# Softmax minus one-hot on one core: whole stores in two transfers, and the load behind them held until the first has landed

## The chip, the cores and the metric

The kernel runs on one core of a Trainium2 chip. The metric is the device time of one execution in microseconds (us). A difference between kernels is measured by running both on the same chip.

## The reference

The input is a batch of logits, 8 x 1024 rows of 8192 float32 values, and one label for each row. For each row the softmax is computed and 1 is subtracted at the label (the gradient of the cross entropy):

```python
def reference(logits, labels):                      # (8, 1024, 8192) f32, (8, 1024) i32
    logits_max = np.max(logits, axis=-1, keepdims=True)
    exp_logits = np.exp(logits - logits_max)
    softmax = exp_logits / np.sum(exp_logits, axis=-1, keepdims=True)
    ...
    one_hot[batch_idx, seq_idx, labels] = 1.0
    return (softmax - one_hot).astype(np.float32)
```

268 MB are read and 268 MB are written.

## The kernel before

The 8192 rows are cut into `B` = 32 batches of 256 rows. A batch has two rows in each of the 128 partitions (`G` = 2), and these two rows follow one another in memory, so that each partition's share of a batch is one run of 64 KB. The buffer `X` has three slots (`SLOTS`) of one batch each. A batch is computed in its slot and stored from it.

For each row t of 64 (`T`, two per batch), VectorE takes the negated maximum (`row_max`), ScalarE the exponentials in place with their sum (`exponentials`), VectorE the reciprocal and, in one instruction, the product less the one-hot row (`finish`). The one-hot row stands as bytes in the PSUM tile `hot`, which ScalarE writes with two instructions per row (`mark`), the first of them through the tile `away`. TensorE only transposes the labels at the start.

Semaphores and their waits are written by hand. The helper `run` (its instructions carry line 77) puts every wait but the last on the engine ahead of the instruction, and the last on the instruction itself. All loads and stores are issued by SyncE, in the order of the program, and go into one queue: `load(b)` waits until the store of batch b - 3, which used the same slot, has landed; `store(b)` waits until the batch's rows are finished.

The strings `LOADS` and `STORES` say for each batch whether it moves row by row ("r", two transfers of 4 MB) or whole ("w", one transfer of 8 MB). The loads of batches 6 to 30 and the stores of batches 3 to 27 are whole. The last batch is stored in four transfers of 2 MB.

The main loop computes batch b, issues its store, and then issues the next load. After batch 3 (`EARLY`) it issues none, so that from then on the load behind store b is that of batch b + 2; its slot was that of batch b - 1. After batch 27 (`LATE`) it issues two.

```python
        for b in range(B):
            work(b)
            store(b)
            if b == EARLY:
                continue
            for _ in range(2 if b == LATE else 1):
                if nxt < B:
                    load(nxt)
                    nxt += 1
```

A transfer over 128 partitions is spread over 16 DMA engines, and its semaphore has its full count when all 16 have landed their share.

Of the kernel before, what the change touches and what calls it, by code (L numbers as in the profile page):

```python
# [8 lines left out]
G = 2  # L9
SLOTS = 3  # L10
EARLY = 3
LATE = 27

LOADS = "rrrrrrwwwwwwwwwwwwwwwwwwwwwwwwwr"
STORES = "rrrwwwwwwwwwwwwwwwwwwwwwwwwwrrrr"
# [3 lines left out]
def kernel(  # L19
# [6 lines left out]
    nc = tc.nc  # L26
# [10 lines left out]
    N, V = x_nv.shape  # L37
# [5 lines left out]
    o_b = o_nv.rearrange("(b p j) v -> b p j v", p=P, j=G)  # L43
# [4 lines left out]
    X = const.tile([P, SLOTS, G, V], fp32)  # L48
# [16 lines left out]
    with tc.tile_critical():  # L65
        sem = tc.alloc_semaphore
        got = [[sem(f"got{i}{q}") for q in range(4)] for i in range(SLOTS)]
        put = [[sem(f"put{i}{q}") for q in range(4)] for i in range(SLOTS)]
# [3 lines left out]
        def run(engine, waits, counter, method, **operands):  # L72

            waits = list(dict.fromkeys(waits))
            for w in waits[:-1]:
                engine.wait_ge(*w)
            instruction = getattr(engine, method)(**operands)  # L77
            for w in waits[-1:]:
                instruction._wait_ge(*w)
            step = 16 if method == "dma_start" else 1  # L80
            instruction.then_inc(counter, step)
            count[counter.name] = count.get(counter.name, 0) + step
            return counter, count[counter.name]

        every, rows = slice(0, P), slice(0, G)
# [7 lines left out]
        def meets(a, b):  # L93
            sets = [[set(range(*d.indices(n))) for d, n in zip(p, (P, G))] for p in (a, b)]
            return all(x & y for x, y in zip(*sets))

        loaded, stored, sides_done = {}, {}, {}
        maxed, summed, marked, finished, freed = {}, {}, {}, {}, {}

        def load(b):  # L100
            loaded[b] = []
            before = stored.get(b - SLOTS, [])
            for q, piece in enumerate(PIECES[LOADS[b]]):
                ps, js = piece
                free = [w for other, w in before if meets(piece, other)]
                w = run(
                    nc.sync, free, got[b % SLOTS][q], "dma_start",
                    out=X[ps, b % SLOTS, js, :], in_=x_b[b, ps, js, :],
                )
                loaded[b].append((piece, w))  # L110

        def store(b):
            stored[b] = []
            if b == B - 1:
                for t in (T - G, T - 1):
                    j = t % G
                    for i, cs in enumerate(sides):
                        w = run(
                            nc.sync, [sides_done[t][i]], put[b % SLOTS][G * j + i],
                            "dma_start", out=o_b[b, every, one[j], cs], in_=X[every, b % SLOTS, one[j], cs],  # L120
                        )
                        stored[b].append(((every, one[j]), w))
                return
            for q, piece in enumerate(PIECES[STORES[b]]):
                ps, js = piece
                w = run(
                    nc.sync, [finished[b * G + js.stop - 1]], put[b % SLOTS][q], "dma_start",
                    out=o_b[b, ps, js, :], in_=X[ps, b % SLOTS, js, :],
                )
                stored[b].append((piece, w))  # L130
# [47 lines left out]

        w_raw = run(nc.scalar, [], lab_got, "dma_start", out=lab_raw[:], in_=lab_bp)
        for b in range(SLOTS):  # L180
            load(b)
        w = run(nc.gpsimd, [], pool, "memset", ap=ident[:], constant=0.0)
        w_ident = run(
            nc.gpsimd, [w], pool, "affine_select",
            out=ident[:], in_=ident[:], compare_op=Alu.not_equal, fill=1.0,
# [8 lines left out]
        for j in range(G):  # L194
            w = run(
                nc.tensor, [w_ident, w_lab], pe, "transpose",
                out=lab_ps[:, j, :], in_=lab_f[:, j, :], identity=ident[:],
            )
        w = run(nc.vector, [w], dve, "tensor_copy", out=lab[:], in_=lab_ps)
        w = run(  # L200
            nc.vector, [w], dve, "tensor_scalar",
            out=part[:], in0=lab[:], scalar1=2, scalar2=None, op0=Alu.arith_shift_right,
        )
        w_word = run(
            nc.vector, [w], dve, "tensor_scalar",
            out=word[:], in0=part[:], scalar1=-1.0, scalar2=None, op0=Alu.mult,
        )
        w = run(
            nc.vector, [w_word], dve, "tensor_scalar",
            out=lab[:], in0=lab[:], scalar1=3, scalar2=None, op0=Alu.bitwise_and,  # L210
        )
        w = run(
            nc.vector, [w], dve, "tensor_copy", out=minus[:], in_=lab[:]
        )
        powers = [256.0**k for k in range(4)]
        w = run(
            nc.vector, [w], dve, "tensor_scalar",
            out=unit[:], in0=minus[:], scalar1=0.0, scalar2=powers[0], op0=Alu.is_equal, op1=Alu.mult,
        )
        for k in (1, 2, 3):  # L220
            w = run(
                nc.vector, [w], dve, "tensor_scalar",
                out=part[:].bitcast(fp32), in0=minus[:], scalar1=float(k),
                scalar2=powers[k], op0=Alu.is_equal, op1=Alu.mult,
            )
            w = run(
                nc.vector, [w], dve, "tensor_tensor",
                out=unit[:], in0=unit[:], in1=part[:].bitcast(fp32), op=Alu.add,
            )
        made_dve = run(  # L230
            nc.vector, [w], dve, "tensor_scalar",
            out=minus[:], in0=unit[:], scalar1=-1.0, scalar2=None, op0=Alu.mult,
# [4 lines left out]
        def work(b):  # L237
            t0, t1 = b * G, b * G + 1
            row_max(t0)
            exponentials(t0)  # L240
            if b == 0:
                mark(0)
                mark(1)
            row_max(t1)
            exponentials(t1)
            finish(t0)
            mark(t0 + G)
            finish(t1)
            mark(t1 + G)

        nxt = SLOTS
# [4 lines that stand above are left out]
                continue  # L256
            for _ in range(2 if b == LATE else 1):
                if nxt < B:
                    load(nxt)
                    nxt += 1  # L260
        for b in range(B - SLOTS, B):
            for _, w in stored[b]:
# [31 lines left out]
```

## Time and profile before

| | |
|---|---|
| median of 3 runs | 1264.38 us (1263.45 to 1265.66) |
| profiled execution | 1262.39 us, its span 1260.6 us |
| VectorE busy | 1120.2 us (89%) |
| ScalarE busy | 722.7 us (57%) |
| DMA queue of loads and stores | 99.5% of 16 engines' span |
| data moved | 426 GB/s over the span |

Busy time is what an engine's instructions took; waits are not in it. The DMA share is the time that the queue's packets took, as a share of the span of all 16 engines. In rows of stretches of time, the columns are the stretch and its width in us, the busy us and instructions of TensorE, its weight load, VectorE, ScalarE and GpSimd, the granted TensorE clock, the DMA engines' share and GB/s. Bytes and the time of a packet are counted in the stretch in which it starts, so that in stretches narrower than a packet the share can be over 1. In rows of instructions in order of time, the columns are start, duration, engine, line and instruction, with the idle time before it and what ended that in brackets. "SPq" is SyncE's queue of DMA issues.

### The profile page before, as it was taken

The numbers are of one execution on the slowest core, as the hardware profiler recorded it, in microseconds if no ns is written. First come the engines' busy times: TensorE is split into PE (matmuls) and PEld (weight loads), VectorE is DVE, ScalarE is ACT, GpSimd is POOL, SyncE is SP. The second block draws the span as 40 slices with busy tenths as digits, with TensorE's granted clock in tenths as the row PEclk, the third lists the DMA queues.
The fourth block names the chain that finished last, engine by engine and source line by source line (L and its number), as shares of the span: only waits on it lengthen the run. The fifth ranks groups of instructions, "written<-read, shape, count | busy, mean of one in ns | idle before, by whom it ended". The sixth has DMA issues, their size and how long they took to land.

```text
span 1260.6 us, 747 instructions
## 1 busy us (share of the span) xinstructions
PE 0.4 (0%) x2; PEld 0.3 (0%) x2; DVE 1120.2 (89%) x208; ACT 722.7 (57%) x257; POOL 2.3 (0%) x7
## 2 busy tenths in 40 slices
PE   0000000000000000000000000000000000000000
PEld 0000000000000000000000000000000000000000
DVE  6899999688988889888898888988889888898995
ACT  3666676356655575545755547555475554755662
POOL 0000000000000000000000000000000000000000
DMA  9999999999999999999999999999999999999998
GB/s 401 416 433 433 434 448 433 430 433 430 433 430 433 433 420 416 430 433 433 416 443 406 433 433 433 412 420 433 433 433 401 430 433 433 433 433 400 435 432 368
DMA packets 11574, 536.99 MB, mean 426 GB/s; under 512 B 1296, under 2 KB 1296, under 8 KB 1328
## 3 DMA queue, kind: packets, MB, share of 16 engines
q1 hardware_dynamic: 11520, 536.88, 99.5%
q10 hardware_dynamic: 48, 0.07, 0.0%
q14 instruction: 6, 0.05, 0.0%
HBM read 268.50 MB, written 268.44 MB: 426 GB/s over the span
## 4 chain that ended last, share of the span: by engine, by line
DVE 50%; DMA 43%; issue 4%; ACT 2%; SPq 0%
DMA X<-in_logits_dram 43%; DVE X L77 25%; DVE m L77 25%; ACT X L77 1%; DVE r L77 1%; ACT hot L77 0%; SPq L77 0%; ACT away L77 0%; SPq L289 0%; SPq L65 0%
## 5 line engine op out<-in xcount | busy, mean ns | idle before, releaser
L77 DVE TENSOR_REDUCE m<-X 128x1 f32<-128x8192 f32 x64 | 553.0, 8680 | 114.3 <-DMA X<-in_logits_dram 114.3
L77 ACT ACTIVATE X<-X,m 128x8192 f32<-128x8192 f32 x64 | 455.8, 7122 | 308.6 <-DVE m L77 308.6
L77 DVE SCALAR_TENSOR_TENSOR X<-X,r,hot 128x8192 f32<-128x8192 f32 (+1 forms) x66 | 560.1, 8489 | 3.8 <-ACT hot L77 1.6
L77 ACT ACTIVATE away<-count,word 128x2048 bf16<-128x2048 int16 x64 | 128.1, 2001 | 199.1 <-DVE X L77 148.1
L77 ACT ACTIVATE hot<-away,unit,minus 128x2048 int32<-128x2048 bf16 x64 | 131.9, 2061 | 2.1
L77 DVE RECIPROCAL r<-s 128x1 f32<-128x1 f32 x64 | 9.9, 155 | 2.4 <-ACT X L77 2.4
L77 ACT ACTIVATION_READ_ACCUMULATOR X<-X,m 128x1 f32 x64 | 11.9, 186 | 0.0
L77 DVE CAST lab_f<-lab_raw 32x256 f32<-32x256 int32 x1 | 0.4, 372 | 4.9 <-DMA lab_raw<-in_labels_dram 4.9
L77 ACT ACT_TABLE_LOAD x1 | 1.3, 1283 | 3.2 <-POOL count L77 3.2
L77 POOL IOTA count<- 128x2048 int16 x1 | 1.8, 1823 | 0.0
L77 DVE TENSOR_TENSOR unit<-unit,part 128x64 f32<-128x64 f32 x3 | 0.7, 224 | 0.1
L77 DVE CAST lab<-hot 128x64 int32<-128x64 f32 x1 | 0.2, 225 | 0.5 <-PE hot L77 0.5
L77 DVE TENSOR_SCALAR part<-minus 128x64 f32<-128x64 f32 x3 | 0.6, 195 | 0.1
L77 PE MATMUL hot<-ident,lab_f 32*128 32x32 f32 x2 | 0.4, 302 | 5.3 <-DVE lab_f L77 5.3
L77 PEld LDWEIGHTS hot<-ident,lab_f 32*128 32x128 f32 x2 | 0.3, 196 | 5.3 <-DVE lab_f L77 5.3
L77 DVE TENSOR_SCALAR part<-lab 128x64 int32<-128x64 int32 x1 | 0.2, 196 | 0.0
L77 DVE TENSOR_SCALAR word<-part 128x64 f32<-128x64 int32 x1 | 0.2, 195 | 0.0
L77 DVE TENSOR_SCALAR lab<-lab 128x64 int32<-128x64 int32 x1 | 0.2, 195 | 0.0
L77 DVE CAST minus<-lab 128x64 f32<-128x64 int32 x1 | 0.2, 195 | 0.0
L77 DVE TENSOR_SCALAR unit<-minus 128x64 f32<-128x64 f32 x1 | 0.2, 195 | 0.0
L77 DVE TENSOR_SCALAR minus<-unit 128x64 f32<-128x64 f32 x1 | 0.2, 195 | 0.0
L77 POOL TENSOR_SCALAR_AFFINE_SELECT ident<-ident 32x32 f32<-32x32 f32 x1 | 0.2, 203 | 0.1
(5 smaller groups left out, 0.5 us busy)
## 6 DMA issues: line engine op xcount, KB each, us to landing
X<-in_logits_dram SPq DMA_DIRECT2D x14, 4096.0 KB, 19.4
out_dram<-X SPq DMA_DIRECT2D x12, 4096.0 KB, 29.5
out_dram<-X SPq DMA_DIRECT2D x4, 2048.0 KB, 12.2
out_dram<-X SPq DMA_DIRECT2D x25, 23.7
X<-in_logits_dram SPq DMA_DIRECT2D x25, 43.1
lab_raw<-in_labels_dram ACTq DMA_DIRECT2D x1, 64.0 KB, 4.0
```

The source lines that it names most:

```text
L77: instruction = getattr(engine, method)(**operands)
```

## The change

Each whole store goes as two transfers over all partitions: the first takes a partition's 16,384 values but the last 2,048, the second takes those. The load that is issued behind a whole store waits, besides what it waited for, until the first of these two transfers has landed on all engines. Loads behind stores by rows wait for nothing more than before.

```diff
+LAST = 2048
...
-        def load(b):
+        def load(b, behind):
             loaded[b] = []
             before = stored.get(b - SLOTS, [])
+            gate = [stored[behind][0][1]] if stored and STORES[behind] == "w" else []
             for q, piece in enumerate(PIECES[LOADS[b]]):
                 ps, js = piece
                 free = [w for other, w in before if meets(piece, other)]
                 w = run(
-                    nc.sync, free, got[b % SLOTS][q], "dma_start",
+                    nc.sync, free + gate, got[b % SLOTS][q], "dma_start",
                     out=X[ps, b % SLOTS, js, :], in_=x_b[b, ps, js, :],
                 )
...
+            if STORES[b] == "w":
+                src = X[:, b % SLOTS].rearrange("p j v -> p (j v)")
+                dst = o_b[b].rearrange("p j v -> p (j v)")
+                cut = G * V - LAST
+                for q, cs in enumerate([slice(0, cut), slice(cut, G * V)]):
+                    w = run(
+                        nc.sync, [finished[b * G + G - 1]], put[b % SLOTS][q], "dma_start",
+                        out=dst[:, cs], in_=src[:, cs],
+                    )
+                    stored[b].append(((every, rows), w))
+                return
...
         for b in range(SLOTS):
-            load(b)
+            load(b, 0)
...
                 if nxt < B:
-                    load(nxt)
+                    load(nxt, b)
```

## The prediction

> **What bounds the kernel now.** I began with the page: its first line, the busy line, the DMA queue, the chain that ended last, and the issues.
>
> ```profile
> span 1260.6 us, 747 instructions
> PE 0.4 (0%) x2; PEld 0.3 (0%) x2; DVE 1120.2 (89%) x208; ACT 722.7 (57%) x257; POOL 2.3 (0%) x7
> q1 hardware_dynamic: 11520, 536.88, 99.5%
> DVE 50%; DMA 43%; issue 4%; ACT 2%; SPq 0%
> out_dram<-X SPq DMA_DIRECT2D x25, 23.7
> X<-in_logits_dram SPq DMA_DIRECT2D x25, 43.1
> ```
>
> The chain names DVE first, but the queue that carries all loads and stores is occupied for 99.5% of the span, and DVE has 11% left. A load lands 43.1 us after its issue and a store 23.7 us: the load stands behind the store in the same queue and two transfers pass before it lands. So the 25 stores and 25 loads of 8 MB (the rows without a size; 128 partitions x 64 KB) are the stage to read. Next I listed VectorE's groups in the stretch of whole transfers, then SyncE's and VectorE's instructions in order of time.
>
> ```profile
> L77 DVE TENSOR_REDUCE m<-X 128x1 f32<-128x8192 f32 x42 | 362.9, 8681 | 90.5 <-DMA X<-in_logits_dram 90.5
> ...
> 238.16 17.28 DVE L77 TENSOR_REDUCE m<-X 128x1 f32<-128x8192 f32 x2 [10.11 <-DMA X<-in_logits_dram]
> 276.78 17.28 DVE L77 TENSOR_REDUCE m<-X 128x1 f32<-128x8192 f32 x2 [3.64 <-DMA X<-in_logits_dram]
> ...
> 512.13 17.28 DVE L77 TENSOR_REDUCE m<-X 128x1 f32<-128x8192 f32 x2 [3.73 <-DMA X<-in_logits_dram]
> 552.27 17.28 DVE L77 TENSOR_REDUCE m<-X 128x1 f32<-128x8192 f32 x2 [5.15 <-DMA X<-in_logits_dram]
> 591.00 17.28 DVE L77 TENSOR_REDUCE m<-X 128x1 f32<-128x8192 f32 x2 [3.74 <-DMA X<-in_logits_dram]
> ...
> 1102.44 8.69 DVE L77 TENSOR_REDUCE m<-X 128x1 f32<-128x8192 f32 x1 [4.07 <-DMA X<-in_logits_dram]
> ```
>
> The first row counts 42 maxima from 276 to 1102 us, so 21 batches of two rows. Each batch starts when its load lands: (1102.44 - 276.78) / 21 = 39.32 us per batch, of which VectorE waits 90.5 / 21 = 4.3. The batch from 238.16 to 276.78 took only 38.62; others took 40.14 (512.13 to 552.27). As 128 partitions go to 16 DMA engines, each engine moves 8 pieces of 64 KB per transfer, 16 per batch: 38.62 / 16 = 2.41 us a piece. That is the unstalled rate, and the kernel loses 0.70 us per batch against it.
>
> To see where, I asked for narrow stretches of time. There GB/s times width, over 65,536 B, counts the pieces that start.
>
> ```profile
> 548.78:549.15 0.37, 0.00 (x0) 0.00 (x0) 0.00 (x0) 0.37 (x1) 0.00 (x0) 1.00 5.74 2480
> 549.15:551.15 2.00, 0.00 (x0) 0.00 (x0) 0.00 (x0) 1.97 (x2) 0.00 (x0) 1.00 0.00 0
> 551.15:551.60 0.45, 0.00 (x0) 0.00 (x0) 0.00 (x0) 0.16 (x1) 0.00 (x0) 1.00 4.70 2039
> 551.60:551.85 0.25, 0.00 (x0) 0.00 (x0) 0.00 (x0) 0.00 (x0) 0.00 (x0) 1.00 0.00 0
> 551.85:551.95 0.10, 0.00 (x0) 0.00 (x0) 0.00 (x0) 0.00 (x0) 0.00 (x0) 1.00 3.03 1311
> ...
> 587.90:588.10 0.20, 0.00 (x0) 0.00 (x0) 0.00 (x0) 0.20 (x1) 0.00 (x0) 1.00 0.00 0
> 588.10:588.30 0.20, 0.00 (x0) 0.00 (x0) 0.00 (x0) 0.20 (x1) 0.00 (x0) 1.00 12.36 5243
> ```
>
> 2480 x 0.37 is 14 pieces; 1311 x 0.10 is 2. Fourteen engines pass from the load to the store at about 549.0; two follow at 551.9, some 2.9 us later, and the load counts as landed only then (VectorE starts at 552.27). The other 2.9 us are worthless to the kernel: fourteen engines run ahead, and pay it back waiting, as at 587.90, where nothing starts until the store issued at 587.29 brings sixteen pieces at once.
>
> **The split.** 25 stores become a transfer of 14,336 columns and one of 2,048, a share of 1/8: per engine 8 pieces of 56 KB, then 8 of 8 KB. No row shows 8 KB pieces. The nearest are the last stores of the kernel, in pieces of 16 KB, against pieces of 32 KB just before:
>
> ```profile
> 1193.00:1207.50 14.50, 0.00 (x0) 0.00 (x0) 14.43 (x5) 11.28 (x4) 0.00 (x0) 1.00 1.01 434
> 1241.08:1255.64 14.56, 0.00 (x0) 0.00 (x0) 5.43 (x2) 0.00 (x0) 0.00 (x0) 1.00 1.00 430
> ```
>
> 434 to 430 is 1%, some 6 ns on a 605 ns piece. Eight more pieces per engine cost 0.05 us a store, 25 x 0.05 = 1.2 us. Bounds: nothing (the difference is partly the edges of the stretches), or four times as much. I take 0.05, the row's own. By the Trainium skill, "DMA: Bandwidth & Descriptors", section "Bandwidth", a 1 MB transfer takes 6.15 us and 16 MB run at 425 GB/s; by that table the tail of 1 MB would cost about 3.7 us more per store, 92 us in all, as an estimate. The trace speaks against it for a queue that is already running: stores of 2 MB pass back to back at 430. The second store instruction on SyncE adds a third of a microsecond there, while the queue still holds work.
>
> **The wait.** Load b+2 was issued right behind store b. Now SyncE holds it until the first part has landed on all sixteen engines. Behind the waiting load on SyncE stands only store b+1, due a batch (39 us) after store b; the wait ends some 21 us after it, so no store is late. The later double issue, after batch 27, already waits for a whole store. ACT and VectorE issue nothing behind it.
>
> The price is a hole in the queue if the way from "first part written" to "load's first piece" is longer than the tail, 19.3 / 8 = 2.4 us. The early stretch, where transfers go by single rows (32 KB pieces), shows this way:
>
> ```profile
> 82.50 0.34 SPq L77 DMA_DIRECT2D X<-in_logits_dram  x1
> 111.19 0.34 SPq L77 DMA_DIRECT2D X<-in_logits_dram  x1
> 150.29 10.24 SPq L77 DMA_DIRECT2D X<-in_logits_dram  x2
> ...
> 80.00:80.40 0.40, 0.00 (x0) 0.00 (x0) 0.40 (x1) 0.40 (x1) 0.00 (x0) 1.00 3.03 1311
> 81.22:81.62 0.40, 0.00 (x0) 0.00 (x0) 0.40 (x1) 0.40 (x1) 0.00 (x0) 1.00 3.07 1311
> ...
> 110.30:110.85 0.55, 0.00 (x0) 0.00 (x0) 0.55 (x1) 0.55 (x1) 0.00 (x0) 1.00 2.22 953
> ...
> 587.29 0.33 SPq L77 DMA_DIRECT2D out_dram<-X  x1
> ```
>
> 953 x 0.55 is sixteen pieces of 32 KB, and so is 1311 x 0.40. At 110.85 all sixteen engines have gone on from a store to the store behind it, and the load that waits for the first is issued at 111.19: 0.34 us. Where a load followed the store, it was 0.9 (81.62 to 82.50). From issue to first piece it was 0.8 to 1.0 (587.29 to 588.10 to 588.30). So the way is 1.1 to 1.9 us, and I take 1.3, since here too a store follows the store. The slowest engine has 1.1 us to spare and loses nothing; an engine ahead of it by over 1.1 us stops for the rest. **So the wait costs the path nothing and caps the lead at 1.1 us at each load's start**, where it was 2.9.
>
> **What that is worth.** The same early rows run in this order already: a load goes out when a store has landed everywhere, with another store as cover. Their batch is 111.19 to 150.29 = 39.10, and the loads' issue before, 72.27 to 111.19, gives 38.92; mean 39.0. Against 39.32 that is 0.31 less, and with the split 0.26: 25 x 0.26 = 6.5 us. The bounds: 38.62 + 0.05, the unstalled batch, saves 0.65 x 25 = 16 us; at the other end nothing is saved. I take the early rows because they are nearest in order of issue, though their pieces are half as long.
>
> ```profile
> 72.27 10.57 SPq L77 DMA_DIRECT2D X<-in_logits_dram  x2
> ```
>
> The profiled execution took 1262.39 us (span 1260.6); the median of the three runs is 1264.38, 2.0 above. The difference is taken from the median: 1264.4 - 6.5 = **1257.9 us**. VectorE takes 35.0 of a batch's 39.0, so it does not become the bound.
>
> **Rival A: all engines turn together and collide (slower).** Where fourteen engines turn from store to load in step, their last piece runs long:
>
> ```profile
> 605.00:605.30 0.30, 0.00 (x0) 0.00 (x0) 0.30 (x1) 0.30 (x1) 0.00 (x0) 1.00 10.30 3495
> 607.40:607.50 0.10, 0.00 (x0) 0.00 (x0) 0.10 (x1) 0.00 (x0) 0.00 (x0) 1.00 3.02 1311
> 607.50:608.05 0.55, 0.00 (x0) 0.00 (x0) 0.55 (x1) 0.00 (x0) 0.00 (x0) 1.00 0.00 0
> 608.05:608.70 0.65, 0.00 (x0) 0.00 (x0) 0.61 (x3) 0.39 (x1) 0.00 (x0) 1.00 3.48 1412
> ```
>
> Sixteen pieces start at 605.00 to 605.30; two engines go on 2.4 us later, the other fourteen only at 608.05 to 608.70, so 0.3 to 1.3 us late, about 0.8. Today that falls on engines that have time. With the lead capped it would fall on the slowest too: 39.0 + 0.05 + 0.8 = 39.85, 0.53 above today, 25 x 0.53 = 13 us, **1277.6**. It decides above 0.26 us per batch on the slowest engine. For it: the trace has it. Against it: at 81.22 to 81.62 sixteen engines turn together from store to load one 32 KB piece after 80.00 to 80.40, with no delay, and the last pieces of the new store are 8 KB.
>
> **Rival B: the lag returns within each load (no change).** A lead of 1.1 us may be enough for the two late engines to be held up when the others turn to the store, as at 549 to 552. Then the batch stays at 39.32 + 0.05: 1264.4 + 1.2 = **1265.6**.
>
> **Rival C: the way is longer than the tail.** If it takes 2.6 us, all engines stand 0.2 us per batch: 39.0 + 0.05 + 0.2 = 39.25, **1262.6**. The rows above (at most 1.9) speak against it. The Trainium skill, same page, section "Anatomy of one DMA", puts about 2.0 us of fixed cost on a transfer, mostly its completion, and 0.6 us to the first byte of the next ("Latency and other measured facts"), which is this case; the rows show 0.34 to 0.9 for the completion.
>
> That the gate does nothing is excluded: today the load is issued 0.4 us after its store, 20 us before the new condition can hold.
>
> **How the numbers follow.** The forecast case 0.47, A 0.35, B 0.12, C 0.06. The three runs spread over 2.2 us, so 0.2% (2.5 us) is what can be told from no change. The forecast case reaches from 1250 (most of its 16 us) to just below the runs of before; A from 1267, where it can first be told from no change, to 1278. I set 1251 to 1277, which leaves out the ends of both. Faster 0.47; same 0.17 (B, C less than 2.5 us away); slower 0.36. The likeliest sign's own range is 1251 to 1262.
>
> **What would show it.** VectorE's maxima should start 39.05 us apart in the stretch of 8 MB transfers, with its wait for loads down from 4.3 to about 4.0 us a batch. SyncE's loads should be issued about 21 us after their stores, not 0.4. In narrow stretches, the sixteen pieces that open a load should start within 1.1 us. Maxima 39.8 us apart with all sixteen engines late at the turn would show A; an unchanged 39.3 with two late engines, B; a stretch in which no engine starts or runs a piece between tail and load, C. A tail above 2.6 us would make the split's price wrong.

## The result, and the profile after

The changed kernel is slower: 1309.33 us (1308.4 to 1309.5) against 1264.59 us, a ratio of 1.0356 with a 95% interval of 1.0343 to 1.0369. That is 44.7 us, 1.8 us for each of the 25 loads that wait.

The page after, with the lines that answer to those of before:

```profile
span 1307.6 us, 797 instructions
PE 0.4 (0%) x2; PEld 0.3 (0%) x2; DVE 1120.2 (86%) x208; ACT 722.9 (55%) x257; POOL 2.3 (0%) x7
q1 hardware_dynamic: 15120, 536.88, 97.5%
DVE 48%; DMA 45%; issue 4%; ACT 2%; SPq 0%
out_dram<-X SPq DMA_DIRECT2D x25, 7168.0 KB, 23.6
out_dram<-X SPq DMA_DIRECT2D x25, 1024.0 KB, 25.7
X<-in_logits_dram SPq DMA_DIRECT2D x25, 24.7
```

The engines' work is the same to 0.2 us; the queue now stands still for 2.5% of the span. The load's time from issue to landing is 24.7 us, where tail and load without any hold-up need 2.1 + 19.3 + 0.4 = 21.8 us (the rest of the tail at the issue, 8 pieces of 2.42 us, and the landing). So a load loses about 3 us on its way (the 24.7 us are a median).

Instructions of VectorE and SyncE in order of time (start, duration, engine and instruction, idle time before and its end):

```profile
241.80 17.28 DVE L78 TENSOR_REDUCE m<-X 128x1 f32<-128x8192 f32 x2 [13.71 <-DMA X<-in_logits_dram]
...
530.16 17.28 DVE L78 TENSOR_REDUCE m<-X 128x1 f32<-128x8192 f32 x2 [6.91 <-DMA X<-in_logits_dram]
572.66 17.28 DVE L78 TENSOR_REDUCE m<-X 128x1 f32<-128x8192 f32 x2 [7.51 <-DMA X<-in_logits_dram]
612.62 8.69 DVE L78 TENSOR_REDUCE m<-X 128x1 f32<-128x8192 f32 x1 [4.97 <-DMA X<-in_logits_dram]
...
1147.53 17.28 DVE L78 TENSOR_REDUCE m<-X 128x1 f32<-128x8192 f32 x2 [4.23 <-DMA X<-in_logits_dram]
...
523.29 0.82 SPq L78 DMA_DIRECT2D out_dram<-X  x2
547.14 0.34 SPq L78 DMA_DIRECT2D X<-in_logits_dram  x1
565.18 0.81 SPq L78 DMA_DIRECT2D out_dram<-X  x2
589.63 0.34 SPq L78 DMA_DIRECT2D X<-in_logits_dram  x1
```

From 241.80 to 1147.53 lie 22 batches: 41.17 us each, against 39.32 before. The load goes out 23.9 us after its store (523.29 to 547.14). Narrow stretches of this load show both of its ends:

```profile
547.14:548.10 0.96, 0.00 (x0) 0.00 (x0) 0.93 (x3) 0.62 (x1) 0.00 (x0) 1.00 0.22 94
548.10:549.25 1.15, 0.00 (x0) 0.00 (x0) 1.15 (x1) 1.15 (x1) 0.00 (x0) 1.00 2.63 912
549.25:550.50 1.25, 0.00 (x0) 0.00 (x0) 1.25 (x1) 1.25 (x1) 0.00 (x0) 1.00 0.00 0
550.50:550.60 0.10, 0.00 (x0) 0.00 (x0) 0.10 (x1) 0.10 (x1) 0.00 (x0) 1.00 2.27 655
551.05:551.85 0.80, 0.00 (x0) 0.00 (x0) 0.80 (x1) 0.80 (x1) 0.00 (x0) 1.00 2.84 1229
...
565.75:566.30 0.55, 0.00 (x0) 0.00 (x0) 0.00 (x0) 0.55 (x1) 0.00 (x0) 1.00 5.48 1907
566.30:568.45 2.15, 0.00 (x0) 0.00 (x0) 0.00 (x0) 2.12 (x2) 0.00 (x0) 1.00 0.00 0
568.45:569.30 0.85, 0.00 (x0) 0.00 (x0) 0.00 (x0) 0.85 (x1) 0.00 (x0) 1.00 2.03 877
569.60:570.00 0.40, 0.00 (x0) 0.00 (x0) 0.00 (x0) 0.00 (x0) 0.00 (x0) 1.00 1.04 451
```

After the issue at 547.14 only 94 GB/s of small tail pieces start: most engines have run out. The load opens at 548.10; 912 x 1.15 is 15 pieces of 64 KB and 8 of the tail. The sixteenth engine opens at 550.5, 3.4 us after the issue, though its tail was over by 549.25. The second pieces start at 551.05 to 551.85, so first pieces took about 3.0 us instead of 2.42. At the other end sixteen pieces start at 565.75 to 566.30: the last ones of fifteen engines and the last but one of the sixteenth, which opened 2.4 us behind. They end not at 568.2 to 568.7 but at 568.45 to 570.00, where 13 pieces of the next store start, then two more and one of 64 KB, the late engine's last. VectorE starts at 572.66, when that one has landed.

Over the loads that waited, the first pieces are 0.64 us too long on average and the last ones 0.62 (worked out from the packets of the trace; in the kernel before 0.08 and 0.06). By the same packets an engine stands idle 1.2 us on average before such a load. The three make 2.5 us a batch. A batch of the kernel before loses some 0.6 us in other places, so 1.9 remain, against 1.85 measured.

### The profile page after: what moved, and what is told of

The parts are those of the page before. It is cut to its first block, busy times and chain, and to the rows that moved or that the text cites. A ratio compares the mean times of both kernels' runs of the same rounds, so it can differ in the third digit from the quotient of the medians.

```text
span 1307.6 us, 797 instructions
## 1 busy us (share of the span) xinstructions
PE 0.4 (0%) x2; PEld 0.3 (0%) x2; DVE 1120.2 (86%) x208; ACT 722.9 (55%) x257; POOL 2.3 (0%) x7
## 4 chain that ended last, share of the span: by engine, by line
DVE 48%; DMA 45%; issue 4%; ACT 2%; SPq 0%
DVE X L78 24%; DVE m L78 24%; DMA X<-in_logits_dram 23%; DMA out_dram<-X 22%; ACT X L78 1%; DVE r L78 0%; ACT hot L78 0%; ACT away L78 0%; SPq L302 0%; SPq L66 0%
## 6 DMA issues: line engine op xcount, KB each, us to landing
out_dram<-X SPq DMA_DIRECT2D x4, 2048.0 KB, 12.3
X<-in_logits_dram SPq DMA_DIRECT2D x25, 24.7
```

## The experiments

All ratios are against the kernel before on the same chip.

**The split alone.** The wait is taken out.

```diff
-                    nc.sync, free + gate, got[b % SLOTS][q], "dma_start",
+                    nc.sync, free, got[b % SLOTS][q], "dma_start",
```

> The split stays, the wait is taken out: the load is issued right behind the store again. Three theories. LATE: the load's pieces reach the engines too shortly before their tail ends, so that an engine opens the load cold (its first piece 0.65 us long on average, some engines 1.3 us late). IN STEP: all sixteen engines turning from store to load and back together costs this, however early the transfer behind is queued. SMALL PIECES: the tail of 8 KB pieces costs it. LATE and IN STEP expect 1266 us (before plus 1.2), SMALL PIECES expects most of the loss to stay, 1295 us or more.

Measured: 1263.91 us, ratio 1.0002 (0.9991 to 1.0012). The split costs nothing that can be told; the loss is the wait's.

**More cover: tails of 4096 and 8192 columns.**

```diff
-LAST = 2048
+LAST = 4096      # and 8192
```

> LAST is 4096 instead of 2048: the load is issued 2.4 us earlier against the end of the tail, the engines' lead is capped at about 3.5 us instead of 1.1, the tail goes in 16 KB pieces. LATE: first pieces of the load back at 2.42 us, 1266 to 1272 us. IN STEP: the engines are still held at each load, and they paid in the changed kernel even where they were 3 us apart at the load's end, so 1290 us or more. SMALL PIECES: half of the loss, about 1287 us.

> LAST is 8192, the second half of the store: the load is issued some 8.5 us before the tail ends, the lead is capped at 8.5 us, which is no cap. All three theories expect the time of before, 1264 to 1267 us; a time well above would mean that the wait costs even where the load comes in good time, which none of them explains.

Measured: 1267.25 us (1.0026, 1.0016 to 1.0036) and 1265.37 us (1.0012, 1.0002 to 1.0021). With 2.4 us more cover 42 of the 45 us are back. First pieces of the load: 0.42 us too long with 4096, 0.08 with 8192. A load that comes in good time costs next to nothing. IN STEP, with its 1290 us, is wrong.

**No cover.** The store is one transfer again, and the load waits for all of it.

```diff
-            if STORES[b] == "w":
+            if False:
```

> The store goes as one transfer again and the load waits for the whole of it: no cover at all. The way from the store's last piece to the load's first is 0.34 to 0.9 us of landing and 1.0 us from issue to first piece, so every engine stands 1.3 to 1.9 us per batch. LATE: the cold opening of the changed kernel is already paid there, the hole comes on top less the 1.1 us that the slowest engine had to spare: 41.3 + 0.3 to 1.0 per batch, 1317 to 1335 us. IN STEP: all engines turn exactly together, the collision at its largest: 39.0 + 1.9 + 1.3 = 42.2 and more, 1332 us or more. If the uneven opening is what costs (engines between 1 and 3 us apart), this kernel opens evenly and could be faster than the changed one, below 1309 us.

Measured: 1339.96 us (1.0596, 1.058 to 1.0612), above LATE's upper end and where IN STEP put it; taken alone it speaks for IN STEP, which the longer tails had ruled out. The last pieces of the load were now 1.21 us too long, more than in the changed kernel. That end of the load became the next question: it might depend on when the next store is queued.

**A later store, by work that nobody needs.** Two additions on a scratch tile ahead of each whole store of the changed kernel; five in the version without a tail.

```diff
             finish(t1)
+            if STORES[b] == "w":
+                w = w_idle
+                for _ in range(2):          # 5 without a tail
+                    w = run(
+                        nc.vector, [w], dve, "tensor_tensor",
+                        out=idle[:], in0=idle[:], in1=idle[:], op=Alu.add,
+                    )
+                finished[t1] = w
```

> The changed kernel with two small additions on a scratch tile (640 columns, about 0.7 us each) on VectorE ahead of every whole store, so that the store is issued about 1.4 us later; they compute nothing that is used. STORE EARLY: most load pieces are then under way when the store arrives, the last pieces fall from 0.62 us too long to 0.1 to 0.3, and the kernel with more work is faster than the changed one by 8 to 13 us: about 1297 to 1301 us. IN STEP or no connection: 1309 to 1315 us.

> The version without a tail (load behind the whole store, 1340 us) with five such additions, about 3.5 us, ahead of every whole store. STORE EARLY: the last pieces of the load, 1.21 us too long on average, fall to below 0.3: about 25 us less, 1312 to 1322 us. IN STEP: engines are as close together as before, 1340 us or more.

Measured: 1272.37 us (1.0068, 1.0048 to 1.0089) and 1314.53 us (1.04, 1.0385 to 1.0416). More work on VectorE took 37 us off the changed kernel, three times what was expected, and 25 off the other, as expected. The last pieces are back at 2.43 us. In narrow stretches and VectorE's maxima of the first of the two:

```profile
594.20:595.05 0.85, 0.00 (x0) 0.00 (x0) 0.82 (x2) 0.85 (x1) 0.00 (x0) 1.00 2.87 1234
595.05:596.65 1.60, 0.00 (x0) 0.00 (x0) 0.19 (x1) 1.57 (x2) 0.00 (x0) 1.00 0.00 0
596.65:597.47 0.82, 0.00 (x0) 0.00 (x0) 0.00 (x0) 0.82 (x1) 0.00 (x0) 1.00 2.59 1119
...
558.66 17.28 DVE L79 TENSOR_REDUCE m<-X 128x1 f32<-128x8192 f32 x2 [2.44 <-DMA X<-in_logits_dram]
597.82 17.28 DVE L79 TENSOR_REDUCE m<-X 128x1 f32<-128x8192 f32 x2 [2.58 <-DMA X<-in_logits_dram]
637.07 8.69 DVE L79 TENSOR_REDUCE m<-X 128x1 f32<-128x8192 f32 x1 [2.67 <-DMA X<-in_logits_dram]
```

1234 x 0.85 is sixteen load pieces, 1119 x 0.82 sixteen pieces of 56 KB: all engines turn within 0.85 us, none late. The batch is 39.2 us, here and in most of the stretch. So here the engines are as close together as the change meant them to be, and turning together costs nothing where the store is issued (595.27) only after the last pieces have started; nor does it bring more than 0.1 us against the 39.32 of before. The extra gain over the forecast came because engines that are not scattered at the load's end also reach the next opening together, with work still in hand: by the packets they stand idle 0.4 us on average before a load instead of 1.2.

**One maximum less.**

```diff
-                nc.scalar, [maxed[t]], act, "activation",
-                out=row(t), in_=row(t), func=Act.Exp, bias=m[:, t : t + 1], scale=1.0,
+                nc.scalar, [*here.values(), maxed[t // G * G]], act, "activation",
+                out=row(t), in_=row(t), func=Act.Exp, bias=m[:, t // G * G : t // G * G + 1], scale=1.0,
...
-            row_max(t1)
```

> The kernel before with one of the two maxima left out: both rows of a partition are shifted by the first row's maximum (the softmax is the same, the computed rows differ only in rounding). The store is issued 8.7 us earlier against its load, so it is queued long before the load behind which it stands has ended. STORE EARLY (a load's last piece runs long when the next store is already queued as it starts; in the changed kernel 0.62 us on average, without a tail 1.21, in the kernel before 0.06): the kernel gets slower although it computes less, by 0.3 to 0.8 us per batch, 1270 to 1285 us. IN STEP (the last piece runs long because all engines turn together): nothing added, the idle moments of the fourteen early engines go, 1250 to 1264 us.

Measured: 1259.51 us (0.9965, 0.9952 to 0.9978). The expectation had the size of the step wrong: the exponentials set the order, and the store moved by 1.2 us, not 8.7. It was no test of an early store, but 1.2 us earlier already gained 4 us.

**An early store, without and with the wait.** In batches 3 to 27 the second row's product is left out; the store waits for the first row's product and the exponentials.

```diff
-            finish(t1)
+            if STORES[b] == "w":
+                finished[t1] = finished[t0]
+                freed[t1] = marked[t1]
+            else:
+                finish(t1)
```

> The kernel before with the second row's product left out in batches 3 to 27 (its rows are stored as exponentials, so that part of the output is not the softmax): the store is issued about 9 us earlier. (Leaving out a maximum moved it only 1.2 us, since the exponentials set the order; that run did not test this.) STORE EARLY without more: last load pieces 0.5 us or more too long on average, 1270 to 1280 us. If a store that is queued early costs only where a gate has brought the engines close together, the early engines' idle moments go and nothing is added: 1250 to 1260 us.

> The changed kernel with the same product left out, the store about 9 us earlier. STORE EARLY: the last pieces of the load go from 0.62 us too long to the 1.2 us of the version without a tail, 1309 + 25 x 0.6 = 1324 us, slower although it computes less. If the moment of the store does not matter, 1309 us or less.

Measured: 1251.18 us (0.9896, 0.9881 to 0.991) without the wait, 1317.04 us (1.0416, 1.0398 to 1.0434) with it. The same edit gains 13 us in one and loses 8 in the other. With the wait, the last pieces are 1.12 us too long, as expected, though the time came out 7 us below 1324; without it 0.08. Without it:

```profile
590.08 17.28 DVE L77 TENSOR_REDUCE m<-X 128x1 f32<-128x8192 f32 x2 [13.41 <-DMA X<-in_logits_dram]
628.78 17.28 DVE L77 TENSOR_REDUCE m<-X 128x1 f32<-128x8192 f32 x2 [12.58 <-DMA X<-in_logits_dram]
667.38 17.28 DVE L77 TENSOR_REDUCE m<-X 128x1 f32<-128x8192 f32 x2 [12.46 <-DMA X<-in_logits_dram]
...
576.74 0.33 SPq L77 DMA_DIRECT2D out_dram<-X  x1
```

38.6 to 38.7 us per batch, the unstalled rate. The store is issued at 576.74, 13.3 us before the load ahead of it lands (590.06); in the kernel before it was 5.1 in the batch of 547.15 to 552.25, and 3.6 to 5.1 for the stores of batches 6 to 27. And the engines are further apart than in the kernel before: up to 5.5 us between the first and the last to land a load, against 1.4 to 3.3 (from the landings in the traces). The lead costs nothing.

**Rows instead of whole transfers.**

```diff
-LOADS = "rrrrrrwwwwwwwwwwwwwwwwwwwwwwwwwr"
+LOADS = "rrrrrrrrrrrrrrrrrrrrrrrrrrrrrrrr"
-STORES = "rrrwwwwwwwwwwwwwwwwwwwwwwwwwrrrr"      # in the first of the two only
+STORES = "rrrrrrrrrrrrrrrrrrrrrrrrrrrrrrrr"
```

> The kernel before with every load and store by rows (pieces of 32 KB, twice as many transfers, no split and no wait for the store behind). The early stretch by rows took 39.0 us per batch against 39.32 in the stretch of whole transfers. If the rows' shorter pieces are what made it so: 39.0 throughout, 1264 - 22 x 0.3 = 1257 us. If it was the early part's small lead of some engines over others, which no gate made: the lead grows here too, 1264 us. More than 1267 us would mean that shorter pieces cost more at the turns.

> The kernel before with all loads by rows and the stores as they were (the version with both by rows took 1253.2 us). If the loads' 64 KB pieces at the turns are what costs (the first piece of a load and the last), most of the 10.6 us gain is here: 1253 to 1257 us. If it is the stores' pieces, 1261 to 1264 us.

Measured: 1253.19 us (0.9917, 0.9902 to 0.9931) with both by rows, 1250.55 us (0.9889, 0.9873 to 0.9906) with the loads alone, both faster than either reading expected. The second is the fastest kernel of this study that computes everything, 14 us faster than before. Piece size is one reading; the profile shows another:

```profile
577.08 0.34 SPq L77 DMA_DIRECT2D out_dram<-X  x1
...
579.67 8.69 DVE L77 TENSOR_REDUCE m<-X 128x1 f32<-128x8192 f32 x1 [2.62 <-DMA X<-in_logits_dram]
589.36 8.69 DVE L77 TENSOR_REDUCE m<-X 128x1 f32<-128x8192 f32 x1 [1.01 <-DMA X<-in_logits_dram]
```

A batch starts when its first row has landed, 9.7 us before the second, and so its store goes out with 12.3 us of load still to come (577.08 to 589.34).

**Piece size alone.** Whole transfers, but in pieces of 32 KB.

```diff
-    X = const.tile([P, SLOTS, G, V], fp32)
+    X_all = const.tile([P, SLOTS, G, V + 16], fp32)
+    X = X_all[:, :, :, :V]
```

> The kernel before with 16 unused columns behind each row in the buffer X, so that a whole transfer keeps its size of 8 MB but goes in pieces of 32 KB instead of 64 KB. If the piece size is what made the version by rows faster: 1253 to 1256 us. If it was the order (the first row's store going 8.7 us earlier, twice as many transfers in the queue): 1262 to 1265 us.

Measured: 1266.92 us (1.0024, 1.0015 to 1.0033). Piece size is not it. What is left is the earlier start, which the early store shares, and that a load goes as two transfers, which no run separates from it.

**The wait beside loads by rows.**

> The changed kernel with all loads by rows (without split and wait that version took 1250.6 us, the fastest so far): both rows' loads wait for the store's first part. LATE: the load's first pieces still open cold; the store is issued while half the load is still to come, as with the early store, so the turn at the load's end costs too: 1250.6 + 25 x 2 to 2.6 = 1300 to 1316 us. If pieces of 32 KB are too short to be held up at the turns: below 1280 us.

Measured: 1317.92 us (1.0421, 1.0397 to 1.0445), just above LATE's range. Pieces of 32 KB are held up as well.

**The wait at every fifth store.** Early store as above; the gate only where `behind % 5 == 0`.

> The changed kernel with the early store (second row's product left out in batches 3 to 27, so that part of the output is not the softmax), but only the loads behind stores 5, 10, 15, 20 and 25 wait for the first part; the others are issued right behind their store. With all gates this took 1317 us, with none (and no split) 1251. NOTHING BEHIND (a load's last piece runs long where only a store, and no load behind it, is queued after it): only the five gated batches lose, 1251 + 5 x 2.6 = 1264 us, and free batches right behind them have last pieces of 2.42 us. IN STEP (it runs long because the gate has brought the engines close together): the free batches behind each gate lose on their last pieces too, until the engines are 4 us apart again, some two batches of 1.1 us for each gate, 1275 us.

Measured: 1270.11 us (1.005, 1.0035 to 1.0065), between the two. A gated load's last pieces (first three rows) and those of the free load behind it:

```profile
471.40:472.00 0.60, 0.00 (x0) 0.00 (x0) 0.00 (x0) 0.00 (x0) 0.00 (x0) 1.00 5.80 1748
472.00:475.00 3.00, 0.00 (x0) 0.00 (x0) 0.00 (x0) 0.00 (x0) 0.00 (x0) 1.00 0.09 38
475.00:475.55 0.55, 0.00 (x0) 0.00 (x0) 0.00 (x0) 0.00 (x0) 0.00 (x0) 1.00 3.38 1460
511.04:512.30 1.26, 0.00 (x0) 0.00 (x0) 0.00 (x0) 0.00 (x0) 0.00 (x0) 1.00 2.18 833
512.30:513.85 1.55, 0.00 (x0) 0.00 (x0) 0.00 (x0) 0.00 (x0) 0.00 (x0) 1.00 0.00 0
513.85:515.45 1.60, 0.00 (x0) 0.00 (x0) 0.00 (x0) 0.00 (x0) 0.00 (x0) 1.00 1.33 573
```

Sixteen pieces that start at 471.40 to 472.00 take 3.0 to 3.8 us; sixteen that start at 511.04 to 512.30 take 2.5 to 3.2. The five gated loads average 1.06 to 1.23 us too long, the free ones 0.0 to 0.5, with 0.8 to 2.8 us between the engines at the landing of the gated and 0.9 to 4.0 of the free. So closeness is at most a small part. NOTHING BEHIND is wrong as a mechanism too: another load was already queued behind the store while the gated load ended.

**The wait on every load, none opened cold.** Early store, a tail of 8192 columns.

> The changed kernel with the early store (second row's product left out in batches 3 to 27, so that part of the output is not the softmax) and a tail of 8192 columns: every load still waits for the first part, but arrives some 8 us before its engines run out. With a tail of 2048 this took 1317 us, without wait and split 1251. In the last run the loads that had waited ran 1.1 us too long on their last pieces, the free ones 0.0 to 0.5, at the same distance between engines and with another load queued behind both. COLD (a load that an engine opens without work before it runs long at both ends): none is opened cold here, 1250 to 1256 us. HELD (that the load waited at all, or came into the queue apart from its store, is the cause): last pieces still 0.6 us or more too long, 1266 us or more.

Measured: 1253.91 us (0.9932, 0.9915 to 0.9948), inside COLD's range. First pieces 0.00 us too long, last ones 0.00 to 0.38. The wait as such costs little: 0.9932 against 0.9896 for the early store without split and wait, 4.5 us over 25 loads. A load that comes only as its engines run out costs, at both ends.

COLD's wording, an engine without work, is too narrow, though. In the changed kernel with the early store more than a quarter of the engines went from their last tail piece straight to the load, and their last pieces are 1.03 us too long all the same (from the packets). The stores of the kernel before show this end of it too:

```profile
565.60:566.10 0.50, 0.00 (x0) 0.00 (x0) 0.50 (x1) 0.50 (x1) 0.00 (x0) 1.00 4.39 1835
568.15:568.60 0.45, 0.00 (x0) 0.00 (x0) 0.45 (x1) 0.06 (x1) 0.00 (x0) 1.00 4.77 2039
```

Both rows are fourteen pieces: the last ones of the store issued at 547.15 take 2.5 us. That store's pieces had started at about 549.0, some 1.9 us after its issue. The store issued at 587.29 opened 0.8 to 1.0 us after its issue, and its last pieces are those of 605.00 to 608.70 in the prediction, about 0.8 us late. Fourteen engines turned within 0.7 us of one another both times, so turning together is not what sets the cost. It goes with the time between issue and opening: of the stores of batches 6 to 26, those that open within 1.2 us have last pieces 0.47 to 0.68 us too long, those that open after 2 us or more 0.06 or less (from the packets). With one maximum less hardly any engine ran out before a store, and it is the same: 0.54 us where a store opened after 1.1 us, 0.02 after 2.2. No run varied this time alone.

## Why the prediction was wrong

- **The split** was forecast at 1.2 us; alone it cost 0.25 us (the interval reaches 1.5). The 92 us that the Trainium skill's "DMA: Bandwidth & Descriptors" gave for a tail of 1 MB as an estimate, from a table of loads that GpSimd issues, did not appear, as the trace had it.
- **What is queued behind the wait**: right. No store came late through SyncE.
- **"The wait costs the path nothing"** is the step that failed. The way was taken as 1.3 us, of which 0.8 to 1.0 from issue to first piece came from a *store's* opening, 587.29 to 588.30, and as one value for all engines. For the first engine that was about right (0.36 + 1.0), for the others not: a load that comes as its engines run out ("cold") opens 1.0 to 3.7 us after its issue, an engine stands idle 1.2 us on average before it, and its first piece is 0.64 us longer. With 2.4 us of cover this did not fit, with 4.8 nearly. The forecast also had no term for the end of the load, where cold-opened loads lose 0.6 to 1.2 us more if the store comes before their last pieces.
- **The cap on the lead** (1.1 us) did not hold: the engines landed 0.7 to 3.8 us apart, because of these delays.
- **"What that is worth"** rested on a wrong cause. The 0.7 us per batch was read as the price of the lead. With leads of 4 to 6.5 us batches take 38.7 us (early store and loads by rows in most of the stretch, early store with the long tail in its last batches). What these share is a store issued 12 to 13 us before the load ahead of it lands, where it was 3.6 to 5.1. In the kernel before, fourteen engines are within 2 us of running out when it comes; the rows of 587.90 to 588.30 showed just this and were read as a consequence only. (The sixteen pieces there are not all of the store: two are the last of the load, which landed at 590.98.) By the packets, the last pieces of its stores lose 0.33 us a batch there, the first pieces of loads and stores 0.1, idle engines somewhat less than 0.1; with the early store these are gone. The largest of them stood in Rival A's rows and was put aside as falling on engines that have time. That the batch in step is 39.05 was nearly right (39.2 with the later store), but batches without a wait came to 39.32 and, with more work in the queue, to 38.7.
- **Rival A** had the sign, and the long last pieces that it saw are real. Its cause for them does not hold: sixteen engines turned within 0.85 us at no cost with the later store, and fourteen in the kernel before turned within 0.5 us, the load long queued, and lost 0.1 us (565.60 to 568.60). Its price of 0.53 us per batch fell short of 1.85. **Rival C** was nearest to the cause, a way longer than the tail, but was priced as a plain hole of 0.2 us and thought refuted by rows of loads that were not cold or of stores. The Trainium skill's 2.0 + 0.6 us in "Anatomy of one DMA" (there for transfers that GpSimd issues) and "Latency and other measured facts" came nearer to the way of the slower engines, 0.36 + 2.8 us for the last one on average, than the 1.3 us taken from rows. Its 0.6 agrees with the 0.63 us at best from the end of a load's issue, which takes 0.34 us, to its first piece; the landing of 0.36 behind a store is shorter than its 2.0.

Open: why a load or store that comes as its engines run out, or shortly before, loses at its *end*, 17 us after it has opened, and, as the loads show, only if the next transfer is queued before its last pieces start.

## What to carry to other kernels

A queue that is never empty is worth more than engines in step: before adding a wait ahead of a transfer, sum the whole way to a *cold* opening of that same kind of transfer, with the spread between engines, and give cover to match; here 4.8 us of it still cost 3 us in all, 9.7 us cost 1.5. When transfers bound the kernel, ask how much work is left in the queue on its fastest engine when the next one is issued; here a store issued 12 us before the load ahead of it landed gave the full rate, and 4 to 5 us (2 on the early engines) cost 1.7% of a batch. An edit that issues a store earlier can gain in one arrangement and lose in another, so it is tried in the arrangement that stays.

## What the runs showed of the hardware that was not expected

- From the issue of a load to its first piece it takes 0.97 to 1.0 us at best on an engine without work, but up to 3.7 us in the changed kernel, it seems on engines that ran out about 1 to 2 us after the issue (if idle engines open in the order in which they ran out).
- A load opened cold has first pieces 0.5 to 0.65 us too long and last ones 0.6 to 1.2, in 64 KB pieces; in 32 KB pieces the last two are some 0.5 us too long each. The last ones are hardly too long at all if the store arrives while they are under way (0.02 and 0.01 with the later store).
- In the kernel before, the last pieces of a store are 0.47 to 0.68 us too long if it opens within 1.2 us of its issue, 0.06 or less after 2 us; with one maximum less it is the same although hardly any engine runs out.
- Sixteen engines drifted 6.5 us apart (early store with the long tail) while batches took 38.7 us, the unstalled rate.
